# A one-core f32 transformer pair: every stage's two operand tiles begin at other bytes

## The chip, the cores and the metric

The kernel runs on one NeuronCore of one Trainium2 chip. The metric is the device time in microseconds of one execution, lower is better.

## The reference, cut to what matters

Two blocks run one after the other on a sequence of 256 tokens with 1,024 features, all in f32. What matters here is that nearly all work is a matrix product with a large weight, and that most products read one normalised activation.

```python
# first block
h = rmsnorm(x, g_mix[l]); proj = h @ w_in[l]          # attention, LRU, memory, gates
merged = g0*(attn_out @ p_attn) + g1*(lru_out @ p_lru) + g2*(mem_out @ p_mem)
x = x + merged @ w_out[l]
h2 = rmsnorm(x, g_ffn[l])
q = (h2 @ w_peer_q) ...                                # top-16 experts of 16384 per head
act = gelu(einsum('chkd,cd->chk', u_tab[ix], hx)); out = einsum('chk,chkd->cd', gx*act, v_tab[ix])
# second block, layer 0: gated_deltanet_bidir; layer 1: dilated_window_attention
for i in range(2):
    x = x + mixer_i(rmsnorm(x, norm_mix[i]))
    h = rmsnorm(x, norm_mlp[i]); x = x + square(relu(h @ w1[i])) @ w2[i]
return rmsnorm(x, norm_final)
```

The kernel computes the expert layer densely: all 16,384 rows of `peer_u` and of `peer_v` pass through TensorE, and the gates pick from the result.

## The kernel before, in words

Activations lie feature-major: a tile `[128, 8, 256]` holds 8 slices (`kt`) of 128 features by T = 256 tokens, so one slice is 1,024 bytes in each partition. Every product is made of three f32r matmuls (`mm3`, L445): both factors are split in a high and a low part, and high·high, high·low and low·high are added in PSUM. The *stationary* operand of a matmul is a 128 x 128 piece of a weight (`whi`, `wlo`, made from `wraw` by ACT at L202 and by DVE or POOL at L206 and L204, streamed from HBM by SP); the *moving* operand is a slice of an activation tile, 256 columns. `gemm_y` (L453) runs over the 8 slices of one activation tile for one output tile `mmps`; `gemm_k` (L486) keeps one slice as the moving operand and fills 8 outputs in the four `acc` banks. The only exceptions among the big products are `d_v`, `w_va` and `w_vm`: there a piece of the weight moves (256, 384 or 512 columns) and the activation stands.

The activation's two parts lie in the pool `opr` under two tags, `xhi` and `xlo`, one buffer each, 8,192 bytes in each partition. Stage after stage takes the same two buffers under other names: `xhi/xlo` (input projections and gates, here stage A), `qhi/qlo` (queries of the experts, Q), `bhi/blo` (`peer_u`, U), `chi/clo` (`peer_v`, V), `ghi/glo` (gated delta net, G), `mxh/mxl` (the two MLPs, M0 and M1), `dxh/dxl` (dilated attention, D), and at the very end `y`. Other moving operands are tiles of their own: `rh/rl` in the second product of an MLP, `yhl` in the output product of the delta net, and the branch results that give `p` and `acc<-mg` in the first block (also called `bhi/blo` there, with output `p`). The stage's tiles are written by `split` (L438): ACT writes the high part (L439), DVE the low part (L441, or L443 with the norm's gain). In stage V the eight slices are rewritten in turn while the products run.

In the program as built, `xhi` begins at byte 67,680 of a partition and `xlo` at byte 75,872. Both are 96 modulo 128 and also 96 modulo 256, and so is every slice, a slice being 1,024 bytes. `whi` and `wlo` begin at 64 modulo 256. `rh`, `rl`, `yhl` and `mg` begin at 160 modulo 256, the branch results of `p` and the tiles of `acc<-dohi` at 32 modulo 256 (all of these are 32 modulo 128).

Of the kernel before, what the change touches and what calls it, by code (L numbers as in the profile page):

```python
# [10 lines left out]
F32 = mybir.dt.float32  # L11
F32R = mybir.dt.float32r
# [10 lines left out]
T = 256  # L23
# [339 lines left out]
def build(tc, a, out, stop=None, dbg=None):  # L363
# [3 lines left out]
    with ctx:  # L367
# [5 lines left out]
        opr = ctx.enter_context(tc.tile_pool(name="opr", bufs=1))  # L373
# [64 lines left out]
        def split(hi, lo, src, scale=1.0):  # L438
            S.activation(hi, src, AF.Copy, scale=scale)  # L439
            if isinstance(scale, float) and scale == 1.0:  # L440
                return V.tensor_sub(lo, src, hi.bitcast(F32)).ins  # L441
            else:
                return V.scalar_tensor_tensor(lo, src, scale, hi.bitcast(F32), op0=ALU.mult, op1=ALU.subtract).ins  # L443

        def mm3(o, whi_, wlo_, xhi_, xlo_, start, stop):  # L445
            mm(o, whi_, xhi_, start, False)
            mm(o, whi_, xlo_, False, False)
            mm(o, wlo_, xhi_, False, stop)

        def aux(nm="aux"):  # L450
            return aux_p.tile([128, 512], F32, name=nm, tag="aux")

        def gemm_y(key, X, kts=range(8), ps=None, first=True, last=True):  # L453
            hi, lo = st.get(key) if key is not None else st.of
            if ps is None:
                ps = mm_p.tile([128, 512], F32, name="mmps", tag="mm")[:, :T]
            kts = list(kts)
            for j, kt in enumerate(kts):
                w = slice(kt * 128, (kt + 1) * 128)
                mm3(ps, hi[:, w], lo[:, w], X[0][:, kt, :], X[1][:, kt, :],  # L460
                    first and j == 0, last and j == len(kts) - 1)
            return ps

        def start(keys, X, after, between, bank=None, half=4):

            ps = [gemm_y(keys[0], X)]
            c = after()
            ps.append(gemm_y(keys[1], X, range(half), last=False))
            r = between(c)
            gemm_y(None, X, range(half, 8), ps[1], first=False)  # L470
            return ps + [gemm_y(keys[2], X, ps=(aux("y3") if bank is None else bank)[:, :T])], r

        def acc_new():
            return [q for _ in range(2) for q in acc_two()]
# [11 lines left out]
        def gemm_k(key, xh, xl, acc, first, last):  # L486
            hi, lo = st.get(key)
            for n in range(8):
                w = slice(n * 128, (n + 1) * 128)
                o = acc[n // 2][:, (n % 2) * T:(n % 2) * T + T]  # L490
                mm3(o, hi[:, w], lo[:, w], xh, xl, first and n % 2 == 0, last)

        def gemm_k2(keys, xs, acc):

            ws = [st.get(k, i == 0) for i, k in enumerate(keys)]
            for n in range(8):
                w = slice(n * 128, (n + 1) * 128)
                o = acc[n // 2][:, (n % 2) * T:(n % 2) * T + T]
                for i in range(2):
                    mm3(o, ws[i][0][:, w], ws[i][1][:, w], *xs[i], False, i == 1)  # L500


        ident = const.tile([128, 128], F32, name="ident")
        make_identity(nc, ident)
# [88 lines left out]
        def plus(x, acc, scale=None):  # L593

            def upd(n):
                q = acc[n // 2][:, (n % 2) * T:(n % 2) * T + T]
                if scale is None:
                    V.tensor_add(x[:, n, :], q, x[:, n, :])
                else:
                    V.scalar_tensor_tensor(x[:, n, :], q, scale, x[:, n, :], op0=ALU.mult, op1=ALU.add)  # L600

            pending.append(upd)

        def operand(x, gname, X, nm, ahead={}):

            N = Norm(nm)
            for kt in range(8):
                update(kt)
                N.lo = split(X[0][:, kt, :], X[1][:, kt, :], x[:, kt, :], col(gname, kt))
                N.add(x[:, kt, :], kt)  # L610
                if kt in ahead:
                    st.pump(cut=ahead[kt])
            return N
# [8 lines left out]
        with ExitStack() as pa:  # L622
# [9 lines left out]
            for i in range(2):  # L632
                nc.sync.dma_start(out=x0[:, 4 * i:4 * i + 4, :], in_=a["xT"][:, 4 * i:4 * i + 4, :])
            st.pump(split=False)
            hx = (opr.tile([128, 8, T], F32R, name="xhi", tag="xhi"), opr.tile([128, 8, T], F32R, name="xlo", tag="xlo"))
            posi = lp.tile([32, T], I32, name="posi", tag="gt", bufs=NG + 1)
            nc.gpsimd.dma_start(out=posi, in_=bass.AP(tensor=a["pos"].tensor, offset=a["pos"].offset, ap=[[0, 32], [1, T]]))
            amask = A1.tile([128, 2, T], F32, name="amask")
# [178 lines left out]
            for c in range(2):  # L817
                hi, lo = st.get(("w_va", c))
                for j in range(4):
                    kt = c * 4 + j  # L820
                    w = slice(j * 256, (j + 1) * 256)
                    for t in range(2):
                        o = vps[:, t * 256:(t + 1) * 256]
# [64 lines left out]
            for n in range(8):  # L888
# [8 lines left out]
                for j in range(8):  # L897
                    w = slice(j * 128, (j + 1) * 128)
                    o = p01[:, :T] if j < 6 else p01[:, T:]
                    mm3(o, hi[:, w], lo[:, w], bo[0][:, j, :], bo[1][:, j, :], j in (0,), j == 5)  # L900
                hi, lo = st.get(("p_all", 2 * n + 1))
                for j in range(8):
                    kt = 8 + j
                    w = slice(j * 128, (j + 1) * 128)
                    o = p01[:, T:] if kt < 12 else p2[:, :T]
# [28 lines left out]


        x1d = dram.tile([128, 8, T], F32, name="x1d")
        hq = (opr.tile([128, 8, T], F32R, name="qhi", tag="xhi"), opr.tile([128, 8, T], F32R, name="qlo", tag="xlo"))
        N = operand(x1, "g_ffn", hq, "ssb")
        nc.gpsimd.dma_start(out=x1d, in_=x1)
        with ExitStack() as pb:  # L940
# [8 lines left out]
            for n in range(16):  # L949
                ps = p3[n] if n < 3 else gemm_y(("w_peer_q", n), hq)  # L950
                V.tensor_mul(qT[:, n, :], ps, rb)
            hb = (opr.tile([128, 8, T], F32R, name="bhi", tag="xhi"), opr.tile([128, 8, T], F32R, name="blo", tag="xlo"))
            for t in range(2):
                for g in range(4):
                    p = aux("sc")
# [144 lines left out]
            bg.drain()  # L1100
            bg.add(scatter(1))
            acc = acc_new()
            cq = (opr.tile([128, 8, T], F32R, name="chi", tag="xhi"), opr.tile([128, 8, T], F32R, name="clo", tag="xlo"))
            cz = []
            for c in range(128):
                if c < 126:
# [23 lines left out]
        with ExitStack() as pc:  # L1130
            C1p = pc.enter_context(tc.tile_pool(name="C1", bufs=1))
            cp = pc.enter_context(tc.tile_pool(name="cp", bufs=2))
            gcs = pc.enter_context(tc.tile_pool(name="gcs", bufs=1))
            hx = (opr.tile([128, 8, T], F32R, name="ghi", tag="xhi"), opr.tile([128, 8, T], F32R, name="glo", tag="xlo"))
            tri = gcs.tile([128, 2, 128], F32, name="tri")
            nc.gpsimd.dma_start(out=tri, in_=a["tri"])

# [405 lines left out]
            for c, h in gorder:  # L1543
# [9 lines left out]
                elif c == "v":  # L1553
                    vf = cp.tile([128, T], F32, name="vf", tag="vf")
                    conv(ps, 16 + h, vf)
                    p = aux("vT")
# [34 lines left out]


        def mlp(i):
            hx = (opr.tile([128, 8, T], F32R, name="mxh", tag="xhi"), opr.tile([128, 8, T], F32R, name="mxl", tag="xlo"))
            N = operand(xr, f"norm_mlp{i}", hx, "ssf")
            acc = acc_new()
            with tc.tile_pool(name="mp", bufs=3) as mp:
                todo = []

                def second():  # L1600
                    n, h, l = todo.pop(0)
                    gemm_k((f"w2_{i}", n), h, l, acc, n == 0, False)

                p3, r2 = start([(f"w1_{i}", n) for n in range(3)], hx, N.sums, lambda c: N.rows(c, "rstd"), half=(YD, YF)[i])
                for n in range(32):
                    ps = p3[n] if n < 3 else gemm_y((f"w1_{i}", n), hx)
                    if n >= LA:
                        second()
                    r = mp.tile([128, T], F32, name="r", tag="r")
                    V.scalar_tensor_tensor(r, ps, 0.0, r2, op0=ALU.max, op1=ALU.mult)  # L1610
                    S.activation(r, r, AF.Square)
                    rh, rl = (mp.tile([128, T], F32R, name=x, tag=x, bufs=LA + 1) for x in ("rh", "rl"))
                    split(rh, rl, r)
                    todo.append((n, rh, rl))
                while len(todo) > 2:
                    second()
                gemm_k2([(f"w2_{i}", n) for n in (30, 31)], [q[1:] for q in todo], acc)
            plus(xr, acc)

        mlp(0)  # L1620
        if stop == "D":
            flush()
# [4 lines left out]
        with ExitStack() as pd:  # L1627
            D1 = pd.enter_context(tc.tile_pool(name="D1", bufs=1))
            dp = pd.enter_context(tc.tile_pool(name="dp", bufs=2))
            hx = (opr.tile([128, 8, T], F32R, name="dxh", tag="xhi"), opr.tile([128, 8, T], F32R, name="dxl", tag="xlo"))  # L1630
            N = operand(xr, "norm_mix1", hx, "ssd", DA)

            vv = D1.tile([128, 2, 1152], F32, name="vv")
# [20 lines left out]
            for j in range(2):  # L1654
                p = aux("trc")
# [16 lines left out]
            for w in (slice(0, 512), slice(512, 768)):  # L1672
                p = aux("bias")
                p = p[:18, :w.stop - w.start]
# [121 lines left out]
        if stop == "E":  # L1796
            flush()
            nc.sync.dma_start(out=out, in_=xr)
            return
        mlp(1)  # L1800
        N = Norm("ssf", V, ND)
        y = opr.tile([128, 8, T], F32, name="y", tag="xhi")
        for kt in range(8):
            update(kt)
            N.add(xr[:, kt, :], kt)
# [32 lines left out]
```

## Time and profile before

| | us |
|---|---|
| median of two runs (1946.83 to 1948.34) | 1947.59 |
| the profiled execution, its own time | 1948.6 |
| its span, first to last instruction | 1946.8 |
| time around the span | 1.8 |
| PE busy | 1851.0 (95%) |
| DVE busy | 1416.4 (73%) |
| ACT busy | 975.0 (50%) |
| mean granted TensorE clock | 0.982 |

How to read it: in a dense stretch each matmul overlaps the next, so its own duration (some 280 ns) is not what it costs. What it costs is the distance from its start to the next one's start, here called the *pace*: a stretch of the chain of waits divided by its matmuls.

### The profile page before, as it was taken

What the parts mean: (1) busy time and instruction counts of PE and PEld (TensorE: products, weight loads), DVE (VectorE), ACT (ScalarE), POOL (GpSimd) and SP (SyncE); (2) the same over time, 40 slices, a digit from 0 to 9 for tenths busy, and PEclk for the clock granted to TensorE, in tenths of its full rate; (3) what the DMA queues carried; (4) which work ended last, traced back from release to release, by engine and by line L of the source; (5) the groups of instructions that cost most, each with busy time, mean ns of one, the idle gap of its engine ahead of it and who ended that gap; (6) DMA issues with size and microseconds to landing.
All of it is one profiled execution on the core that took longest, in us unless ns stands there. A gap on an engine that the chain in (4) does not pass through costs nothing.

```text
span 1946.8 us, 38503 instructions
## 1 busy us (share of the span) xinstructions
PE 1851.0 (95%) x15622; PEld 1812.2 (93%) x15622; DVE 1416.4 (73%) x2644; ACT 975.0 (50%) x1589; POOL 347.5 (18%) x202
## 2 busy tenths in 40 slices
PE   8999999999989999999999997669999999999998
PEld 7989999999989999999999996668899999999998
DVE  7698666877778887999865559997565556766555
ACT  6577444544443334444354454634754546455543
POOL 2010001343433332000000045552130001010000
PEclk9999999999999999999999998889999999999999
DMA  6534556455554445545565662344145566645653
GB/s 225 184 121 141 184 185 208 154 170 181 170 170 152 151 153 162 164 154 162 162 204 188 188 215 80 95 100 104 44 151 184 184 185 204 195 131 184 185 186 108
DMA packets 113703, 314.85 MB, mean 162 GB/s; under 512 B 35042, under 2 KB 38242, under 8 KB 112758
## 3 DMA queue, kind: packets, MB, share of 16 engines
q1 hardware_dynamic: 112390, 305.82, 49.9%
q0 software_dynamic: 1136, 6.59, 1.0%
q8 instruction: 122, 2.00, 0.4%
q14 instruction: 55, 0.45, 0.1%
HBM read 307.06 MB, written 5.30 MB: 160 GB/s over the span
## 4 chain that ended last, share of the span: by engine, by line
PE 80%; DVE 14%; issue 2%; ACT 2%; DMA 0%; POOL 0%; DVEq 0%; SPq 0%; ACTq 0%; POOLq 0%
PE mmps L434 36%; PE acc L434 34%; PE gp L434 3%; DVE cy L1254 3%; DVE wlo L206 2%; PE p L434 2%; PE vps L434 1%; ACT whi L202 1%; DVE U L1291 1%; DVE kv L1337 1%; DVE mxl L443 1%; PE lg L434 1%; DVE tk L1034 1%; PE po L434 0%; DVE tk L1033 0%
## 5 line engine op out<-in xcount | busy, mean ns | idle before, releaser
L202 ACT ACTIVATE whi<-wraw 128x1024 fp32r<-128x1024 f32 x562 | 595.7, 1060 | 785.2 <-PE acc L434 299.6
L206 DVE TENSOR_TENSOR wlo<-wraw,whi 128x1024 fp32r<-128x1024 f32 x461 | 577.7, 1254 | 315.2 <-ACT whi L202 313.3
L204 POOL TENSOR_TENSOR wlo<-wraw,whi 128x1024 fp32r<-128x1024 f32 x101 | 248.8, 2464 | 694.3 <-ACT whi L202 629.0
L434 PE MATMUL mmps<-bhi,wlo 128*128 128x256 f32 x1024 | 286.6, 280 | 8.0 <-DVE wlo L206 7.7
L434 PE MATMUL mmps<-bhi,whi 128*128 128x256 f32 x1024 | 288.8, 282 | 3.7 <-ACT act L1089 3.7
L434 PE MATMUL mmps<-blo,whi 128*128 128x256 f32 x1024 | 286.3, 280 | 0.0
L434 PE MATMUL acc<-chi,whi 128*128 128x256 f32 x1008 | 283.2, 281 | 0.0
L434 PE MATMUL acc<-clo,whi 128*128 128x256 f32 x1008 | 281.2, 279 | 0.3 <-DVE clo L441 0.3
L434 PE MATMUL acc<-chi,wlo 128*128 128x256 f32 x1008 | 280.9, 279 | 0.0
L434 PEld LDWEIGHTS mmps<-bhi,wlo 128*128 128x128 f32 x1024 | 192.5, 188 | 9.4 <-DVE wlo L206 8.7
L434 PEld LDWEIGHTS mmps<-bhi,whi 128*128 128x128 f32 x1024 | 193.2, 189 | 4.3 <-ACT act L1089 4.3
L434 PEld LDWEIGHTS mmps<-blo,whi 128*128 128x128 f32 x1024 | 192.5, 188 | 0.0
L434 PEld LDWEIGHTS acc<-clo,whi 128*128 128x128 f32 x1008 | 189.6, 188 | 0.6 <-DVE clo L441 0.5
L434 PEld LDWEIGHTS acc<-chi,whi 128*128 128x128 f32 x1008 | 189.9, 189 | 0.0
L434 PEld LDWEIGHTS acc<-chi,wlo 128*128 128x128 f32 x1008 | 189.5, 188 | 0.0
L434 PE MATMUL acc<-rl,whi 128*128 128x256 f32 x512 | 144.6, 283 | 0.0
L434 PE MATMUL acc<-rh,wlo 128*128 128x256 f32 x512 | 144.5, 282 | 0.0
L434 PE MATMUL acc<-rh,whi 128*128 128x256 f32 x512 | 143.1, 280 | 0.0
L434 PE MATMUL mmps<-mxl,whi 128*128 128x256 f32 x496 | 140.3, 283 | 1.3 <-DVE mxl L443 1.0
L434 PE MATMUL mmps<-mxh,wlo 128*128 128x256 f32 x496 | 139.6, 281 | 0.8 <-DVE wlo L206 0.8
L434 PE MATMUL mmps<-mxh,whi 128*128 128x256 f32 x496 | 138.9, 281 | 0.8 <-ACT mxh L439 0.5
L434 PE MATMUL mmps<-xhi,whi 128*128 128x256 f32 x384 | 111.3, 290 | 1.7 <-DVE qm L860 1.2
(576 smaller groups left out, 4474.2 us busy)
## 6 DMA issues: line engine op xcount, KB each, us to landing
wraw<-in_peer_u SPq DMA_DIRECT2D x128, 512.0 KB, 3.6
wraw<-in_peer_v SPq DMA_DIRECT2D x128, 512.0 KB, 3.9
wraw<-in_w SPq DMA_DIRECT2D x128, 512.0 KB, 4.3
wraw<-in_w_gates SPq DMA_DIRECT2D x24, 512.0 KB, 3.5
wraw<-in_p_all SPq DMA_DIRECT2D x16, 512.0 KB, 3.6
wraw<-in_w_peer_q SPq DMA_DIRECT2D x16, 512.0 KB, 3.6
wraw<-in_d_v SPq DMA_DIRECT2D x12, 512.0 KB, 4.4
wraw<-in_d_q SPq DMA_DIRECT2D x9, 512.0 KB, 4.3
```

The lines of the kernel that those rows point to most:

```text
L202: nc.scalar.activation(hi, t, AF.Copy)
L204: nc.gpsimd.tensor_tensor(lo, t, hi.bitcast(F32), op=ALU.subtract)
L206: self.lasts.append(nc.vector.tensor_sub(lo, t, hi.bitcast(F32)).ins)
L434: x = PE.matmul(o, l, r, start=start, stop=stop, skip_group_check=True)
L443: return V.scalar_tensor_tensor(lo, src, scale, hi.bitcast(F32), op0=ALU.mult, op1=ALU.subtract).ins
L1034: V.tensor_tensor(eq.rearrange("p (h k) c -> p h k c", h=2), eq.rearrange("p (h k) c -> p h k c", h=2), tif4[:, h:h + 2, p2, None, :].to_b ...
L1254: V.scalar_tensor_tensor(y[:, lo_:hi_], x[:, lo_ + d:hi_ + d], col("gdn_conv", j * 24 + base), y[:, lo_:hi_], op0=ALU.mult, op1=ALU.add)
L1291: V.scalar_tensor_tensor(U[:, u, :], kk[:, h, t, :], rk2b[:, t, d, h:h + 1], D[:, u, :], op0=ALU.mult, op1=ALU.mult)
L1337: V.tensor_tensor(q, M[:, 0:i, 0:i].rearrange("p j c -> p c j"), L[:, i, None, 0:i].to_broadcast([128, i, i]), op=ALU.mult)
```

## The change

A new helper `operands(names, at)` takes the same two buffers, each 32 elements (128 bytes) longer, and returns views that begin `at` bytes in. Each stage calls it with two offsets of its own, all multiples of 4. `y` takes the longer buffer and begins where it did. In the core of the diff below the seven calls stand for the seven lines that they replace.

```diff
+        def operands(names, at):
+            r = []
+            for nm, tag, o in zip(names, ("xhi", "xlo"), at):
+                t = opr.tile([128, 8 * T + 32], F32R, name=nm, tag=tag)
+                r.append(t[:, o // 4:o // 4 + 8 * T].rearrange("p (k t) -> p k t", t=T))
+            return tuple(r)
-            hx = (opr.tile([128, 8, T], F32R, name="xhi", tag="xhi"), opr.tile([128, 8, T], F32R, name="xlo", tag="xlo"))
+            hx = operands(("xhi", "xlo"), (112, 120))
+        hq = operands(("qhi", "qlo"), (16, 24))
+            hb = operands(("bhi", "blo"), (8, 4))
+            cq = operands(("chi", "clo"), (48, 80))
+            hx = operands(("ghi", "glo"), (64, 36))
+            hx = operands(("mxh", "mxl"), ((0, 16), (12, 20))[i])
+            hx = operands(("dxh", "dxl"), (104, 100))
-        y = opr.tile([128, 8, T], F32, name="y", tag="xhi")
+        y = opr.tile([128, 8 * T + 32], F32, name="y", tag="xhi")[:, :8 * T].rearrange("p (k t) -> p k t", t=T)
```

In the program as built the instructions, their order on every engine and their semaphores are the same. The first buffer still begins at byte 67,680; the second moves by 128 bytes to 76,000, and whatever lies behind it in the partition moves by 256 bytes, which leaves its place modulo 256 as it was. The stages' slices then begin here (before: 96 and 96 everywhere):

| stage | matmuls on its tiles | high part, modulo 256 (128) | low part, modulo 256 (128) |
|---|---|---|---|
| A `xhi/xlo` | 1,152 | 208 (80) | 88 (88) |
| Q `qhi/qlo` | 384 | 112 (112) | 248 (120) |
| U `bhi/blo` | 3,072 | 104 (104) | 228 (100) |
| V `chi/clo` | 3,024 | 144 (16) | 48 (48) |
| G `ghi/glo` | 792 | 160 (32) | 4 (4) |
| M0 `mxh/mxl` | 768 | 96 (96) | 240 (112) |
| D `dxh/dxl` | 432 | 200 (72) | 68 (68) |
| M1 `mxh/mxl` | 768 | 108 (108) | 244 (116) |

## Rows read from the trace of the kernel before

**Rows 1.** The page: engines' busy time and instructions; TensorE's granted clock, 40 slices.
```profile
PE 1851.0 (95%) x15622; PEld 1812.2 (93%) x15622; DVE 1416.4 (73%) x2644; ACT 975.0 (50%) x1589; POOL 347.5 (18%) x202
PEclk9999999999999999999999998889999999999999
```

**Rows 2.** The page: the chain that ended last, shares by engine, then by line.
```profile
PE 80%; DVE 14%; issue 2%; ACT 2%; DMA 0%; POOL 0%; DVEq 0%; SPq 0%; ACTq 0%; POOLq 0%
PE mmps L434 36%; PE acc L434 34%; PE gp L434 3%; DVE cy L1254 3%; DVE wlo L206 2%; PE p L434 2%; PE vps L434 1%; ACT whi L202 1%; DVE U L1291 1%; DVE kv L1337 1%; DVE mxl L443 1%; PE lg L434 1%; DVE tk L1034 1%; PE po L434 0%; DVE tk L1033 0%
```

**Rows 3.** Busy time in stretches: A, U, V, G, M0; then clock and DMA.
```profile
core 0: us, PE busy (x) PEld busy (x) DVE busy (x) ACT busy (x) POOL busy (x), PEclk, DMA share, GB/s
34.00:238.00 204.00, 198.41 (x1501) 189.49 (x1500) 162.41 (x328) 130.88 (x227) 10.61 (x8) 0.98 0.50 159
...
339.00:754.00 415.00, 402.92 (x3645) 399.11 (x3644) 327.53 (x787) 183.50 (x275) 158.67 (x64) 1.00 0.50 162
755.00:1141.00 386.00, 385.71 (x3528) 384.19 (x3526) 289.14 (x468) 174.57 (x259) 7.54 (x3) 1.00 0.56 178
1147.00:1389.00 242.00, 191.24 (x1492) 181.85 (x1492) 199.05 (x431) 126.27 (x271) 105.92 (x56) 0.89 0.36 100
1424.00:1612.00 188.00, 186.67 (x1547) 185.50 (x1546) 109.77 (x143) 96.14 (x144) 8.46 (x8) 0.99 0.57 180
```

**Rows 4.** Groups by line and tile, one product of three per stage: busy, mean, idle before.
```profile
L434 PE MATMUL mmps<-bhi,whi 128*128 128x256 f32 x1024 | 288.8, 282 | 3.7 <-ACT act L1089 3.7
L434 PE MATMUL acc<-chi,whi 128*128 128x256 f32 x1008 | 283.2, 281 | 0.0
L434 PE MATMUL mmps<-mxh,whi 128*128 128x256 f32 x496 | 138.9, 281 | 0.8 <-ACT mxh L439 0.5 <-DVE r L1610 0.3
L434 PE MATMUL mmps<-xhi,whi 128*128 128x256 f32 x384 | 111.3, 290 | 1.7 <-DVE qm L860 1.2 <-DVE m L910 0.4
L434 PE MATMUL mmps<-ghi,whi 128*128 128x256 f32 x256 | 79.3, 310 | 9.1 <-DVE cx L1249 9.1
L434 PE MATMUL mmps<-dxh,whi 128*128 128x256 f32 x144 | 41.2, 286 | 0.0
L434 PE MATMUL mmps<-qhi,whi 128*128 128x256 f32 x120 | 33.7, 282 | 0.3 <-ACT qhi L439 0.3
```

**Rows 5.** The chain in order of time, M0: start us, length us, what, matmuls.
```profile
1446.58 2.88 PE acc L434 x24
1449.46 2.83 PE mmps L434 x24
1452.29 2.88 PE acc L434 x24
```

**Rows 6.** The chain elsewhere: `p`, U twice, V's second half, `yhl`, `d_v`.
```profile
229.58 5.67 PE p L434 x48
...
353.62 57.87 PE mmps L434 x490
...
461.72 51.66 PE mmps L434 x443
...
972.33 182.40 PE acc L434 x1560
...
1412.67 15.85 PE acc L434 x132
...
1640.95 8.55 PE vps L434 x48
```

**Rows 7.** The chain at a plain f32 product of 256 columns, stage A.
```profile
65.01 0.86 PE lg L434 x4
```

**Rows 8.** Groups by line: the two writers of stage V's tiles; DVE in an MLP's.
```profile
L441 DVE TENSOR_TENSOR clo<-act,chi 128x256 fp32r<-128x256 f32 x126 | 51.9, 418 | 0.0
L439 ACT ACTIVATE chi<-act 128x256 fp32r<-128x256 f32 x126 | 49.1, 400 | 1.4 <-DVE act L1083 1.4
L443 DVE SCALAR_TENSOR_TENSOR mxl<-xr,cols,mxh 128x256 fp32r<-128x256 f32 x16 | 12.7, 812 | 0.5 <-ACT mxh L439 0.5
```

More of the change, by code (lines that the diff above doesn't have):

```diff
@@ L936, in build @@
         x1d = dram.tile([128, 8, T], F32, name="x1d")
-        hq = (opr.tile([128, 8, T], F32R, name="qhi", tag="xhi"), opr.tile([128, 8, T], F32R, name="qlo", tag="xlo"))
+        hq = operands(("qhi", "qlo"), (16, 24))
         N = operand(x1, "g_ffn", hq, "ssb")
@@ L951, in build @@
                 V.tensor_mul(qT[:, n, :], ps, rb)
-            hb = (opr.tile([128, 8, T], F32R, name="bhi", tag="xhi"), opr.tile([128, 8, T], F32R, name="blo", tag="xlo"))
+            hb = operands(("bhi", "blo"), (8, 4))
             for t in range(2):
@@ L1102, in build @@
             acc = acc_new()
-            cq = (opr.tile([128, 8, T], F32R, name="chi", tag="xhi"), opr.tile([128, 8, T], F32R, name="clo", tag="xlo"))
+            cq = operands(("chi", "clo"), (48, 80))
             cz = []
@@ L1133, in build @@
             gcs = pc.enter_context(tc.tile_pool(name="gcs", bufs=1))
-            hx = (opr.tile([128, 8, T], F32R, name="ghi", tag="xhi"), opr.tile([128, 8, T], F32R, name="glo", tag="xlo"))
+            hx = operands(("ghi", "glo"), (64, 36))
             tri = gcs.tile([128, 2, 128], F32, name="tri")
@@ L1593, in mlp @@
         def mlp(i):
-            hx = (opr.tile([128, 8, T], F32R, name="mxh", tag="xhi"), opr.tile([128, 8, T], F32R, name="mxl", tag="xlo"))
+            hx = operands(("mxh", "mxl"), ((0, 16), (12, 20))[i])
             N = operand(xr, f"norm_mlp{i}", hx, "ssf")
@@ L1629, in build @@
             dp = pd.enter_context(tc.tile_pool(name="dp", bufs=2))
-            hx = (opr.tile([128, 8, T], F32R, name="dxh", tag="xhi"), opr.tile([128, 8, T], F32R, name="dxl", tag="xlo"))
+            hx = operands(("dxh", "dxl"), (104, 100))
             N = operand(xr, "norm_mix1", hx, "ssd", DA)
```

## The prediction

> **What bounds the kernel now.** I read the page's engine line first, then the shares of the chain, then the busy time by stage, and last the chain in order of time, from which the pace comes. [...] The chain that ends last is PE for 80%, and `mmps` and `acc`, the two outputs of the big products, make 70% [rows 2]. By stage the bound is clear where most matmuls are: in U PE works 402.9 of 415 us, in V 385.7 of 386, in M0 186.7 of 188, in A 198.4 of 204. Only in G does it idle, 191 of 242 us, with DVE at 199 [rows 3]. So a change of the pace of matmuls reaches the end almost undiminished in every stage but G, and what ACT, DVE and the DMAs do in between is covered.
>
> The paces are the key. In M0 the chain alternates between two products of the same form: 24 matmuls that write `mmps` take 2.83 us, 117.9 ns each, and 24 that write `acc` take 2.88 us, 120.0 ns each [rows 5]. Clock, sizes, types and the weights' buffers are the same. What differs is the output bank pattern and the start of the moving operand: `mxh/mxl` begin at 96 modulo 256, `rh/rl` at 160. The output pattern is not it: in V, which also writes `acc` but whose slices begin at 96, 1560 matmuls take 182.40 us, 116.9 ns each [rows 6]. And `yhl`, at 160, writes `acc` at 15.85 us for 132, 120.1 ns [rows 6]. So the byte at which a moving operand begins already costs up to 3 ns in 117 in this trace. That 32 modulo 128 is not one class shows too: `p`, at 32 modulo 256, has 5.67 us for 48, 118.1 ns [rows 6], between the two. The start 64 appears where a weight piece of 384 columns moves: 8.55 us for 48 `vps`, 178.1 ns, or 118.7 per 256 columns [rows 6]. So four starts are known, 96, 32, 64 and 160, with 116.6 to 118.1, 118.1, 118.7 and 120.0 ns. At one and the same start the pace also has two values: U runs 490 matmuls in 57.87 us (118.1 ns) and later 443 in 51.66 us (116.6 ns) [rows 6].
>
> **The change part by part.** No instruction is added, removed or moved, no byte more is transferred, and no wait changes; the two buffers grow by 128 bytes a partition. All that can cost is access to the shifted tiles.
>
> *Moving reads.* The groups count 1024, 1008, 496, 384, 256, 144 and 120 matmuls for one of the three products of `mm3` [rows 4]; three times their sum is 10,296 (96 more stand in small groups). G's 768 are left out, for there DVE and not PE ends the chain. In M0 the high part keeps its start, 96, so its 496 (two products of 248) cost nothing. 10,296 - 768 - 496 = 9,032 matmuls read at a new start. What they cost there the trace shows for none of the new starts but G's 160. From below: nothing, or a gain; 96 is the best start of four, but nothing says that it is the best of all. From above, without a new mechanism: the 120.0 ns of the start 160. I take the mean of the three other known starts, since the new ones are spread over the whole 256 bytes: (118.1 + 118.7 + 120.0) / 3 = 118.9 ns. The old pace over U, V and M0 is about 117.1 ns (116.6 and 118.1 in U, 116.9 in V, 117.9 in M0). The difference is 1.8 ns, and 9,032 x 1.8 ns = 16 us. The two paces of U put some 0.75 ns on either side, 7 us.
>
> *Writes and other reads of the shifted tiles.* ACT writes and DVE reads and writes 256 columns at a time: 400 and 418 ns in V, 812 ns in an MLP's norm where DVE waits for ACT [rows 8]. V's 126 pairs have idle engines around them (DVE 289, ACT 175 of 386 us [rows 3]). On the path lie only the seven norms with 8 pairs each; if each pair became 5% slower, (0.4 + 0.8) us x 56 x 0.05 = 3 us. No row shows such a cost, and the shifted f32 elements still lie whole in their 4 bytes, so I take 0.
>
> *Stationary reads.* In D, parts of `dxh/dxl` stand instead of moving. These loads overlap the matmuls before them (PEld 1812 us beside PE's 1851 [rows 1]), and I take 0.
>
> The sum, made against the profiled execution: 1948.6 + 16 = 1965 us. That execution lies 1.0 us above the median of 1947.6; I let the 1 us stand, as it is far inside the spread. If the cover of DVE and ACT were missing the 3 us would come on top.
>
> [...]
>
> **The rivals.**
> *No effect (1943 to 1953 us).* The difference between 96 and 160 could come from where `rh` and `yhl` lie in the partition or how far the parts are from each other, not from the low bits. For it: one start has two paces in U. Against it: `rh`, `yhl` and the output product in the first block lie far apart and all begin at 160. It gives 1948.
>
> *One more piece per slice (slower).* If PE fetches a slice in fixed pieces, a start inside a piece needs one piece more. All four known starts are multiples of 32, so no row speaks against pieces of up to 32 bytes; pieces of 64 would have made 96, 32 and 160 dearer than 64 by a sixteenth, 7.3 ns, which they are not. With 32-byte pieces each of nearly all 9,032 matmuls pays 116.9 / 32 = 3.7 ns, 33 us: 1948.6 + 33 = 1982, and with the 16 us of the spread 1998. With pieces of 16 bytes only those in U, M1, D and the low parts of A and Q pay (some 4,800 matmuls), 1.8 ns each: 9 us, 1957 to 1974. Beyond 39 us, 4.3 ns each, it is slower by over 2%. [...]
>
> *The fast rate is lost (much slower).* A start that is a multiple of 4 but not of 8 could break the pace of f32r. The nearest row is plain f32, where each matmul of 256 columns takes 0.86 us / 4 = 215 ns [rows 7], 98 ns more. Four modulo 8 are the low parts of U (1,024), D (144) and both parts of M1 (744): 1,912 x 98 ns = 187 us, 2136 us. For it speaks only that no moving operand at such a start stands in the trace.
>
> *A gain (faster).* If the new starts were as much better than 96 as 160 is worse, 9,032 x 3.1 ns = 28 us come off: 1920. [...] Faster by over 2% needs -4.3 ns per matmul. Against it: all three other known starts are worse than 96.
>
> **How the numbers follow.** My forecast, a small loss between 1953 and 1980 us: 0.45. No effect: 0.20. A gain: 0.10, of which 0.03 by over 2%. One more piece at 32 bytes, 1980 to 2005: 0.20, of which 0.15 beyond 2% (1986.5). The fast rate lost: 0.05. With 0.02 for a larger spread than seen, slower by over 2% has 0.22, faster 0.03, and 0.75 stay within 2%, about what a measurement of this kernel can tell from no change. The range goes down into the gains, to 1942, and up through most of the 32-byte case, to 2000; below it is about 0.08, above it about 0.12. The likeliest case's own range is 1953 to 1980.
>
> **What would show it.** The chain in order of time gives the pace of each stage again. Right: U, V, A, Q, D and M1 between 117 and 120 ns, V (two thirds of its matmuls at 144) and U setting the sum, M0 least changed, `rh/rl` as before at 120.0, `p` at 118.1, G's chain still DVE's. A uniform 120.5 or more in every stage with starts off a multiple of 32 is the piece rival; stages at 4 modulo 8 near 215 ns for their shifted products are the lost rate; unchanged paces are the first rival. The forecast is wrong if the paces move by different amounts for the same class of start, or if the span moves without them.

## The result, and the profile after

The changed kernel takes 1966.47 us (median of two runs, 1965.88 to 1967.05) against 1947.59 us: ratio 1.0095, 95% interval 1.0076 to 1.0114. That is 18.9 us or 1% slower; 1965 had been forecast. The profiled execution has 1965.88 us and a span of 1964.1 us, 17.3 us more than the span of before.

The page after, with the engines' busy time and the granted clock, is to be set beside [rows 1]:

```profile
PE 1875.8 (96%) x15622; PEld 1835.8 (93%) x15622; DVE 1414.4 (72%) x2644; ACT 974.6 (50%) x1589; POOL 347.6 (18%) x202
PEclk9999999999999999999999998889999999999998
```

The chain of waits after, in order of time (start us, length us, what, matmuls): `p`, U twice, V's second half, `yhl`, then M0 twice, `d_v`, M1 three times; it is to be set beside [rows 5, 6]:

```profile
229.57 5.67 PE p L434 x48
...
354.21 76.19 PE mmps L434 x634
...
464.04 70.41 PE mmps L434 x587
...
985.10 185.70 PE acc L434 x1560
...
1425.68 15.85 PE acc L434 x132
...
1460.95 2.83 PE mmps L434 x24
1463.78 2.88 PE acc L434 x24
...
1652.36 8.42 PE vps L434 x48
...
1768.59 3.83 PE mmps L434 x17
...
1865.77 2.85 PE mmps L434 x24
1868.63 2.88 PE acc L434 x24
```

The other engines worked as long as before, and PE 25 us longer with the same 15,622 matmuls. U now runs at 76.19 / 634 = 120.2 and 119.9 ns a matmul (118.1 and 116.6 before), V at 119.0 (116.9). What the change did not touch stands still to the second decimal: `p` 5.67 us for 48, `yhl` 15.85 for 132, `rh/rl` 2.88 for 24. M0's own product, whose high part keeps its start, has 2.83 for 24 as before.

The stages' lengths, from the first matmul of each stage to the first of the next, tell where the 17 us arose. The pace beside them is the mean distance between starts of all matmuls on the stage's two tiles, distances over 135 ns (a wait) left out:

| stage | length before, us | after | difference | pace before, ns | after |
|---|---|---|---|---|---|
| A | 252.6 | 252.6 | 0.0 | 116.8 | 117.1 |
| Q | 52.0 | 52.7 | +0.7 | 117.8 | 119.9 |
| U | 416.6 | 425.4 | +8.9 | 116.9 | 120.3 |
| V | 392.3 | 398.9 | +6.6 | 116.7 | 118.9 |
| G | 276.8 | 273.8 | -3.1 | 117 | 118.9 |
| M0 | 187.9 | 186.4 | -1.5 | 117.7 | 118.0 |
| D | 127.9 | 129.0 | +1.1 | 117 | 120.8 |
| M1 | 189.6 | 194.3 | +4.7 | 116.6 | 119.1 |

Not all of it is pace. Busy time by stretch after (columns as in [rows 3]); V, G, M0, M1 and M1's first 47 us:

```profile
765.00:1164.00 399.00, 398.71 (x3581) 397.04 (x3580) 291.78 (x470) 177.35 (x261) 7.54 (x3) 1.00 0.55 175
1164.00:1438.00 274.00, 227.37 (x1772) 216.17 (x1772) 216.64 (x471) 147.88 (x316) 122.17 (x69) 0.91 0.35 95
1438.00:1624.00 186.00, 184.68 (x1543) 183.54 (x1542) 110.03 (x144) 95.67 (x144) 8.43 (x8) 1.00 0.58 182
...
1753.00:1947.00 194.00, 192.75 (x1574) 191.22 (x1574) 111.00 (x147) 98.47 (x148) 8.45 (x8) 0.98 0.51 164
...
1753.00:1800.00 47.00, 45.75 (x345) 44.22 (x345) 28.91 (x45) 25.88 (x46) 8.45 (x8) 0.93 0.43 136
```

V is as full as before (398.7 of 399 us), so its pace passes whole to the end. In M1 the granted clock is 0.50 for a while at the norm: the chain there has 17 matmuls in 3.83 us, 225 ns each, where before, at 1.00, it had

```profile
1755.41 2.10 PE mmps L434 x17
```

Before, such a dip lay in M0 (0.99 over the stage [rows 3], 0.59 over 14 matmuls that take 2.87 us, 205 ns each), and in the kernel after M0 has 1.00. So M1 pays some 3 us and M0 gains 1 to 2 that have nothing to do with the operand's place. In G, where PE idles 47 of 274 us, the dearer pace (118.9 against 117) is not seen in the length at all.

### The profile page after: what moved, and what is told of

It reads as the page before. It is cut to its first block, busy times and chain, and to the rows that moved or that the text cites. A ratio compares the mean times of both kernels' runs of the same rounds, so it can differ in the third digit from the quotient of the medians.

```text
span 1964.1 us, 38503 instructions
## 1 busy us (share of the span) xinstructions
PE 1875.8 (96%) x15622; PEld 1835.8 (93%) x15622; DVE 1414.4 (72%) x2644; ACT 974.6 (50%) x1589; POOL 347.6 (18%) x202
## 4 chain that ended last, share of the span: by engine, by line
PE 83%; DVE 13%; ACT 2%; issue 2%; DMA 0%; DVEq 0%; SPq 0%; ACTq 0%
PE mmps L434 38%; PE acc L434 34%; PE gp L434 3%; DVE cy L1262 3%; DVE wlo L206 2%; PE p L434 2%; PE vps L434 1%; DVE U L1299 1%; ACT whi L202 1%; DVE mxl L443 1%; DVE kv L1345 1%; PE lg L434 1%; PE po L434 0%; DVE tk L1042 0%; DVE tk L1041 0%
## 5 line engine op out<-in xcount | busy, mean ns | idle before, releaser
L434 PE MATMUL mmps<-bhi,wlo 128*128 128x256 f32 x1024 | 292.5, 286 | 7.3 <-DVE wlo L206 7.3
L434 PE MATMUL mmps<-bhi,whi 128*128 128x256 f32 x1024 | 293.2, 286 | 3.3 <-ACT act L1097 3.3
L434 PEld LDWEIGHTS acc<-clo,whi 128*128 128x128 f32 x1008 | 189.6, 188 | 0.6 <-DVE clo L441 0.5
```

The source lines that it names most:

```text
L434: x = PE.matmul(o, l, r, start=start, stop=stop, skip_group_check=True)
```

## The experiments

All kernels take the two buffers longer and the helper of the change; a third argument of `operands` is the extra distance between slices in elements, so that V's eight slices can have eight starts. The edits below show the lines that matter; `...` marks lines left out. Starts are given modulo 256; where nothing else is said the weights' parts stay at 64 and high and low part begin at the same place. Each kernel's paces are worked out as in the table above, V's for each slice alone (some 370 matmuls each).

### A grid of 32 bytes, a grid of 4 bytes

`e1_grid32`; the lines of U and V stand here for those of all stages:

```diff
-            hb = operands(("bhi", "blo"), (8, 4))
+            hb = operands(("bhi", "blo"), (64, 64))
...
-            cq = operands(("chi", "clo"), (48, 80))
+            cq = operands(("chi", "clo"), (0, 0), 8)
```

> Both parts of a stage begin at the same byte modulo 256 here, all of them multiples of 32: A 128, Q 0, U 160, M0 64, M1 192, D 224, and stage V's eight slices at 96, 128, 160, 192, 224, 0, 32, 64. The weights stay at 64. Theory 1 (the pace is a property of the start modulo 256): U near 120.0 ns, the pace of rh and yhl at 160, against 116.9 before; V's slices differ among each other, 96 at 116.7, 160 at 120.0, 32 near 118.2, 64 near 118.5; M0 near 118.5. Theory 2 (the pieces: only a start off a multiple of 32, or 16, costs): all stages and all slices within 1 ns of 117. Theory 3 (not the start but the place of rh and yhl in the partition): likewise all at 117, rh at 120. Time: about 1948 us by theories 2 and 3; by theory 1 U alone adds 3072 x 3.1 ns = 9.5 us, V about 1.5 ns on 3024 = 4.5 us, together some 1960 to 1966.

`e2_grid4` is made the same way, with U at 104 and V's slices 4 bytes apart:

```diff
+            hb = operands(("bhi", "blo"), (8, 8))
...
+            cq = operands(("chi", "clo"), (0, 0), 1)
```

> Fine steps: stage V's eight slices begin at 96, 100, 104, 108, 112, 116, 120, 124 modulo 256, and the other stages, both parts alike, at A 200, Q 88, U 104, M0 208, M1 112, D 68. Theory 1 (a property of the start modulo 256, single bytes included): the paces of the changed kernel come back start by start wherever they stand, 104 near 121.6 ns in U and in V's third slice, 112 near 120.6 in M1 and V's fifth, 200 near 120.6 in A, 208 near 116.9 in M0, 68 near 121 in D. Theory 2 (pieces of 16 bytes): V's slices at 96 and 112 alike at 116.7 ns, the six others 1.8 ns higher and alike; with pieces of 32 bytes seven slices alike, 3.7 ns above 96. Theory 4 (what counts is the pair of the high and the low part's starts, 104 with 228 in the changed kernel): U at 104 with 104 far from the 120.3 ns that its stage had. Time: by theory 1 U adds 3072 x 4.5 ns = 14 us, V some 2 ns x 3024 = 6 us, M1 and A 3 to 4 us: 1968 to 1974; by theory 2 at 16 bytes 1955 to 1960.

Measured: 1957.85 us and 1967.18 us (before beside them: 1948.17). V's slices, ns a matmul:

| e1: start | 0 | 32 | 64 | 96 | 128 | 160 | 192 | 224 |
|---|---|---|---|---|---|---|---|---|
| ns | 114.2 | 118.2 | 119.6 | 118.0 | 117.6 | 119.5 | 118.7 | 117.8 |

| e2: start | 96 | 100 | 104 | 108 | 112 | 116 | 120 | 124 |
|---|---|---|---|---|---|---|---|---|
| ns | 116.9 | 121.2 | 120.2 | 117.7 | 118.4 | 120.3 | 119.8 | 116.7 |

The time of e1 lies just below the 1960 to 1966 us expected, that of e2 just below its 1968 to 1974. What follows: the pace depends on the start down to 4 bytes. Pieces of 32 bytes are out: 124, 108 and 208 (M0 in e2 118.9) lie within such a piece and cost no more than 64. The lost fast rate is out too: at 4 modulo 8 the dearest is D at 68 in e2 with 123.1 ns, nowhere near 215. And 96 is not the best: Q at 0 in e1 runs at 113.6 ns.

### Everything 64 bytes further

`e3_shift` puts 64 bytes ahead of all tiles, so the weights begin at 128; the operands of U, V, Q and G move along (96 to 160), those of A, M0, M1 and D stay at 96:

```diff
+        const.tile([128, 16], F32, name="shift")
...
+            hb = operands(("bhi", "blo"), (0, 0))
...
+            hx = operands(("dxh", "dxl"), (192, 192))
```

> Everything in the partition behind the first few tiles lies 64 bytes further on, the weights' two parts included (128 instead of 64 modulo 256). U, V, Q and G keep their old distance to the weights and so begin at 160; A, M0, M1 and D are put back to 96, 32 bytes ahead of the weights' start instead of 32 behind it. rh and yhl lie at 224, p at 96. Theory R (the distance between moving and stationary operand counts, as where two reads meet): U and V stay at 116.9 and 116.7 ns, rh at 120.0, p at 118.2; M0, M1 and A change, to about 118.2, the pace that the distance of -32 had in p. Time about 1948 to 1951 us. Theory 1 (the moving start by itself): U and V go to 120.0 ns, p to 117, rh to what the first scan shows at 224 (117 to 118), M0, M1, A and D stay at 117. Time 1948 + (3072 + 3024) x 3.1 ns = 1967, less 4 us in rh.

Measured: 1952.86 us. The chain, U twice and V's second half:

```profile
355.40 57.87 PE mmps L435 x490
...
463.57 51.66 PE mmps L435 x443
...
975.33 182.40 PE acc L435 x1560
```

These three lengths are those of before to the last digit [rows 6], though every tile begins 64 bytes later and the operand at 160, the start that cost 120.0 in [rows 5]. A, M0, M1 and D, at 96 as before but with the weights at 128, went from 116.6 to 117.7 up to 118.2 and 118.3 ns, the pace that `p` (32, weights at 64) has. So it is not the moving operand's start alone: the start of the standing weights counts as well, and 64 bytes on both together change nothing. U and V carry this; the rise in A, M0, M1 and D is not much more than the 1.1 ns between the two levels that one pair of starts can have (next section).

### One stage alone

`e4_u_alone` gives U its two starts of the change (104 and 228) and all other stages 96:

```diff
+            hb = operands(("bhi", "blo"), (8, 132))
...
+            cq = operands(("chi", "clo"), (0, 0))
```

> Only U has its new starts (104 and 228 modulo 256), every other stage begins at 96 with both parts. If the stages add up, each by its own pace: U at 120.3 ns instead of 116.9, 3072 x 3.4 ns = 10.4 us, of which the stage lengths of the two traces show 8.9; the time 1956 to 1958 us against 1947.6, ratio 1.0045 to 1.0055, and V, M1 and D as before. If the loss came from where the buffers behind the operand tiles lie, or from the stages together, the ratio would be 1.000 or 1.009.

Measured: 1957.74 us (1956.06 to 1958.34), ratio 1.0052, interval 1.0032 to 1.0072. The chain, U and V:

```profile
351.54 76.21 PE mmps L434 x634
...
979.07 184.06 PE acc L434 x1560
```

U has its 76.2 us for 634 as in the changed kernel and is 8.8 us longer, as U is there (8.9); V is back at 117.2 over the stage, with 118.0 in this stretch. U's cost comes through whole when U alone has it; the ratio of 1.009 expected from a common cause did not come.

V here shows something else. Its starts and those of its weights are the ones of before (96 and 64), yet this stretch takes 184.06 us where [rows 6] have 182.40, and V is 1.7 us longer. Taken block by block (24 matmuls on one slice), V has 116.7 ns in its first half and 117.8 in its second, and before it has 116.7 in both. U before begins at 117.8 and stands at 116.7 from about the thirtieth of its 128 blocks on; M0 and M1 have 117.7 and 116.6 before, and 116.6 and 117.7 here. So one pair of starts can have two paces, 1.1 ns apart, and it keeps either for hundreds of matmuls. Nor is that scatter: over a thousand matmuls without a gap in V's second half, the three matmuls of one product take 350.0 ns before, 353.3 in e4 and 356.7 in the changed kernel. What sets the level isn't shown. Differences of about 1 ns between two kernels therefore don't tell two starts apart, while those of 3 ns and more do.

### Where the cheap starts lie

`e5_grid16` sets V's slices to the other multiples of 16 and the stages close above 0; `e6_near0` looks finer around 0.

```diff
+            hb = operands(("bhi", "blo"), (160, 160))
...
+            cq = operands(("chi", "clo"), (16, 16), 8)
```

> The odd multiples of 16: stage V's eight slices begin at 112, 144, 176, 208, 240, 16, 48, 80 modulo 256 (both parts alike); U at 0, the one start that was clearly better than 96 (114.1 ns in V and 113.6 in Q of the first scan); A 4, Q 8, M0 252, M1 248, D 12, all close to 0. Theory R with 256-byte periods (the distance to the weights' start, 64, sets the pace, and -64 is a place where the two reads miss each other): U near 114 ns, 3072 x 2.8 = 9 us off; A, Q, M0, M1 and D each between 112 and 118, lower the nearer they are to the good distance; 112 in V at 118.4 as in the fine scan. The rival (the low pace at 0 belongs to a start on a 256-byte boundary itself, a whole number of pieces, and not to the distance): U at 114 as well, but A at 4, Q at 8, M0 at 252, M1 at 248 and D at 12 lose all of it at once and stand at 118 or more. Time: with U at 114 and the rest near 118, about 1946 to 1952 us.

```diff
+            hb = operands(("bhi", "blo"), (140, 140))
...
+            cq = operands(("chi", "clo"), (136, 136), 2)
```

> Steps of 8 around 0: stage V's eight slices at 232, 240, 248, 0, 8, 16, 24, 32 modulo 256; U 236, A 244, Q 20, M0 16, M1 28, D 176. By the distance to the weights the pace falls from some 118 at 232 to 114 or less near 0 and comes back to 118.2 at 32, over several neighbouring starts; by the rival (a whole number of pieces only at 0) the slice at 0 stands alone at 114 among seven at 118 to 120. Time 1946 to 1960 us.

Measured: 1956.72 us (before beside it 1949.43) and 1965.28 us, both above the times expected (up to 1952 and 1960), since the starts around the cheap 0 came out dear. V's slices:

| e5: start | 16 | 48 | 80 | 112 | 144 | 176 | 208 | 240 |
|---|---|---|---|---|---|---|---|---|
| ns | 119.0 | 117.4 | 115.4 | 118.2 | 119.1 | 114.4 | 118.7 | 119.4 |

| e6: start | 232 | 240 | 248 | 0 | 8 | 16 | 24 | 32 |
|---|---|---|---|---|---|---|---|---|
| ns | 120.0 | 119.2 | 120.1 | 114.9 | 120.1 | 119.1 | 121.5 | 118.2 |

The stages close to 0 in e5 (starts 4, 8, 12, 248 and 252) have 118.3 to 121.7 ns. So there is neither a smooth hollow around 0 nor a single boundary: three lone starts, 0, 80 and 176, are 3 ns cheaper than their neighbours on the grid of 16. D at 176 in e6 has 114.2 again. These means mix V's two halves; in the first, where the products `gp` come between some of its blocks, the cheap starts are dearer (80: 117.1, then 114.0; 176: 115.0, then 113.7). Over the four kernels e1, e2, e5 and e6, multiples of 16 lie between 114 and 120 ns (mean about 118), 8 modulo 16 between 119 and 121.5, 4 modulo 16 between 120 and 123, 12 modulo 16 between 116.7 and 120.

### The cheap start everywhere, and in the two tiles alone

`e8_all176` puts every moving operand at 176, also `rh/rl`, `yhl`, `mg`, the branch results and `dohi/dolo`; `e12_two_tiles` moves the two tiles of each stage only and leaves out the rest:

```diff
+            hb = operands(("bhi", "blo"), (80, 80))
...
+                    rh, rl = (mp.tile([128, T + 64], F32R, name=x, tag=x, bufs=LA + 1)[:, 4:4 + T] for x in ("rh", "rl"))
...
+            mg = A1.tile([128, 8 * T + 64], F32R, name="mg", tag="r12")[:, 4:4 + 8 * T].rearrange("p (a b t) -> p a b t", a=4, b=2)
```

> Weights at 64 as before; every moving operand of the big products at 176 modulo 256: the two tiles of all stages, and also rh/rl, yhl, mg (160 before) and the branch results of p and acc<-dohi (32 before). By the single looks 176 has 114.2 to 114.4 ns in two stages. If 176 holds in all stages: U 3,072 x 2.6 + V 3,024 x 2.3 + A, Q, M0, D, M1 3,500 x 2.7 + rh/rl, yhl, mg some 2,000 x 5.7 + the others 2 us, some 38 us, 1910 us, ratio 0.980. Rival: DVE, ACT or the weights' stream then end more of the waits (before: U 403 of 415 us busy, A 198 of 204), and only a part comes through, 1915 to 1930, ratio 0.984 to 0.991. Rival: the low pace of 176 was of those two stages or of the other parts' places and not of the start: paces of 117, 1945, ratio 0.998.

> Only the two operand tiles at 176 in every stage; rh/rl, yhl, mg, the branch results and dohi/dolo back at their starts of before (a part of e8_all176). The parts add up: e8 gave 39 us; the 1,536 matmuls of rh/rl at 6.7 ns, yhl, mg, p and dohi at 4 to 6 ns are some 15 us of these, which come back: 1924 us, ratio 0.988 (0.986 to 0.990), and paces of 114 in the stages, 120 for rh/rl. Rival: the other tiles' starts cost nothing and the gain of e8 was all in the two tiles: 1909.

Measured: e8 1908.33 us (1906.55 to 1910.22), ratio 0.9806, interval 0.979 to 0.9822, the best kernel of this study. e12 1922.05 us (1920.22 to 1927.54), ratio 0.9877, interval 0.9853 to 0.9902. The page of e8, then its chain: U twice, V, M0:

```profile
PE 1808.0 (95%) x15622; PEld 1769.1 (93%) x15622; DVE 1416.2 (74%) x2644; ACT 976.2 (51%) x1589; POOL 351.2 (18%) x202
```

```profile
352.18 60.16 PE mmps L434 x528
...
452.38 50.28 PE mmps L434 x444
...
956.48 177.49 PE acc L434 x1560
...
1446.48 2.72 PE mmps L434 x24
1449.20 2.72 PE acc L434 x24
```

And the chain of e12, V and M0:

```profile
959.41 177.48 PE acc L434 x1560
...
1447.36 2.88 PE acc L434 x24
1450.24 2.72 PE mmps L434 x24
```

The pair of M0 shows it on four rows: 2.83 and 2.88 before, 2.72 and 2.88 with the two tiles moved, 2.72 and 2.72 with `rh/rl` moved too, 113.3 ns where it was 120.0. With weights at 64, start 176 gives 113.3 to 115.7 ns in every stage. Both times came out as summed from the paces (1910 and 1924 expected); no other engine takes over, DVE stands at 74%.

### The weights 8 and 16 bytes further

Is it the distance between the two starts alone? `e7_weights8` moves the weights to 72, `e10_weights16` to 80; in both the ring of raw weights is one tile shallower (3 instead of 4) to make room.

```diff
-            hi = self.his.tile([128, 1024], F32R, name="whi", tag="whi")
+            hi = self.his.tile([128, 1088], F32R, name="whi", tag="whi")[:, 2:1026]
```

> Weights' parts begin 8 bytes later (72 modulo 256 instead of 64; for that the ring of raw weights is 3 deep instead of 4), and each stage has high and low part at one start: U 104, A 96, M0 8, M1 0, D 184, Q 112, V's eight slices 96, 104 ... 152. Theory of the distance (only moving start minus stationary start counts, modulo 256): U is 32 behind its weights, as 96 was, so 116.9 ns; A (24, as 88) 120; M0 (-64, as 0 was) 114.5; M1 (-72, as 248) 119.7; D (112, as 176) 114.2; V 96: 120.1, 104: 116.8, 112: 120.2, 120: 118.4, 128: 119.8, 136: 117.6. Theory of the start's own place in 16 bytes (multiples of 16 cheap, 8 modulo 16 dear, wherever the weights lie): U 119.5 to 120, A 117, M0 120, M1 115, D 120, V 96 117 and 104 120. rh/rl (160, distance 88, as 152): by distance 120 or a little more, by own place 120.0.

```diff
+            hi = self.his.tile([128, 1088], F32R, name="whi", tag="whi")[:, 4:1028]
```

> Weights' parts begin 16 bytes later (80 modulo 256; the ring of raw weights 3 deep instead of 4). High and low part at one start: A 176, Q, U, D 192, M0 176, M1 96, V's slices 224, 240, 0, 16, 32, 48, 64, 80. Theory of the distance in whole steps of 16 bytes (each start acts as the one 16 bytes lower did before weights at 64): U, Q, D 192 as 176: 114.2; A, M0 176 as 160: 120; M1 96 as 80: 115.4; V 118.7, 117.9, 119.4, 114.5, 119, 118.2, 117.9, 119.6. Theory of the own place: U, Q, D 118.7; A, M0 114.2; M1 116.8; V 117.9, 119.4, 114.5, 119, 118.2, 117.9, 119.6, 115.4. rh/rl (160): by distance as 144, 119; by own place 120.0.

Measured: 1953.67 and 1957.50 us. Paces, with what each theory expected:

| kernel, place, start | measured, ns | by distance | by own place |
|---|---|---|---|
| e7 U 104 | 120.2 | 116.9 | 119.5 to 120 |
| e7 A 96 | 117.9 | 120 | 117 |
| e7 M0 8 | 121.2 | 114.5 | 120 |
| e7 D 184 | 123.4 | 114.2 | 120 |
| e7 Q 112 | 113.5 | 119.3 to 120.2 | 118.3 |
| e7 V 112 | 114.5 | 120.2 | 118.3 |
| e7 M1 0 | 118.2 | 119.7 | 115 |
| e10 A, M0 176 | 119.8, 119.4 | 120 | 114.2 |
| e10 V 16 | 114.2 | 114.5 | 119 |
| e10 V 0 | 118.8 | 119.4 | 114.5 |
| e10 U 192 | 119.1 | 114.2 | 118.7 |
| e10 V 32 | 123.2 | 119 | 118.2 |
| e10 M1 96 | 117.4 | 115.4 | 116.8 |

One row from each chain, M0 in e7 (120.8 ns) and a stretch of U in e10 (120.3):

```profile
1446.71 2.90 PE mmps L434 x24
```

```profile
357.12 60.41 PE mmps L434 x502
```

Both theories fall. `rh/rl`, at 160 in both kernels, say the same: 118.6 ns in e7 and 118.1 in e10, where both theories had 119 or more. By 8 bytes the order of cheap and dear follows mostly the operand's own place in 16 bytes, but a new cheap start appears, 112. By 16 bytes the start 176 loses its low pace and the cheap 0 moves along to 16, while the cheap 176 does not move to 192. Only this stands: the pace belongs to the pair of starts, and a pair must be measured.

### Who meets whom

`e9_no_prep` takes e5's starts for V and 160 for U, and leaves out the preparation of weights in half of U and half of V (which blocks, the expectation says); their products use the parts made last.

```diff
+        def none(i):
+            name, c = self.plan[i][0]
+            return (name == "peer_u" and 64 <= c < 128) or (name == "peer_v" and 4 <= c < 64)
...
+            if none(self.ns):
...
+                self.s[self.ns] = self.kept
```

> Part of the work left out: the 64 last blocks of peer_u are neither loaded nor split (their products take the parts of block 63 again), blocks 4 to 63 of peer_v are loaded but not split. U's tiles begin at 160, V's slices at 16, 48, 80 ... 240 as in e5_grid16. Theory one (TensorE's own two reads, moving and stationary, meet in the memory): the paces stay: U 120.0 in both halves, V 119.0, 117.4, 115.4, 118.2, 119.0, 114.4, 118.7, 119.4 in both halves. Theory two (TensorE's reads meet those and the writes of DVE, ACT, POOL or of the DMAs on the weights): in U's second half, where none is left, and largely in V's first half, the paces of all starts fall to the 113 to 114.5 of start 176, and come back in V's second half. If only V's first half stays dear, it is the DMAs alone.

Measured: 1959.25 us. Busy time by stretch (columns as in [rows 3]): U's first half, U's second, V's first, V's second:

```profile
360.00:540.00 180.00, 175.06 (x1449) 173.81 (x1447) 138.17 (x469) 87.53 (x128) 74.08 (x30) 1.00 0.54 170
560.00:755.00 195.00, 195.00 (x1860) 193.44 (x1859) 105.54 (x239) 21.65 (x56) 0.00 (x0) 1.00 0.50 160
790.00:970.00 180.00, 180.00 (x1718) 178.80 (x1718) 104.23 (x240) 21.41 (x51) 0.00 (x0) 1.00 0.01 1
985.00:1150.00 165.00, 165.00 (x1406) 165.00 (x1406) 93.09 (x124) 82.51 (x124) 6.99 (x2) 1.00 0.61 189
```

The transfers of the blocks that are loaded but not split ran ahead, through U's second half; in V's first half there is then none (0.01), POOL has no instruction and ACT works 21 of 180 us. The paces did not fall: U 119.98 and 119.94 ns in its halves; V's slices in the first half 119.0, 117.4, 116.6, 118.3, 118.3, 115.2, 118.6, 119.6 and in the second 119.0, 117.4, 114.0, 118.2, 119.6, 113.7, 118.8, 119.2 (starts 16, 48 to 240). e5, with all the preparation, has the same difference between its halves at 80 and 176, so the first half is dearer there with or without it. So the DMAs, POOL and ACT don't set these paces; they stayed, as theory one has it, but its cause, two reads that meet, isn't shown by that. DVE, with 104 of 180 us, was still there, so this kernel does not take its part away. The traces do, though: in V's second half before (980 to 1145 us), the 692 distances between starts during which DVE works throughout average 116.67 ns, the 604 during which it idles 116.70; in e8 (965 to 1130 us) it is 113.31 over 758 and 113.33 over 558. DVE's work beside a matmul doesn't change the pace either. Where the loaded weights begin does: M0 and A at 176 have 119.4 and 119.8 ns with weights at 80 (e10), 113.5 and 114.3 with weights at 64 (e8), and U and V at 160 have 116.6 to 118.1 ns with weights at 128 (e3), where U at 160 has 119.94 to 119.98 with weights at 64 (e9).

### Two starts in one stage

The change gives each stage two starts; e1 to e8 mostly one. `e11_mixed` mixes starts whose paces were known alone:

```diff
+            hb = operands(("bhi", "blo"), (0, 64))
...
+            cq = operands(("chi", "clo"), (80, 0))
```

> Weights at 64 as before, high part / low part at two different starts, each known from stages where both parts began there: A 160/96, Q 176/160, U 96/160, V 176/96, M0 176/0, M1 0/176, D 176/96. Two of three products read the high part. Theory one (each matmul has the pace of its own start, so different starts cost nothing in themselves): A (2 x 120 + 117) / 3 = 119, Q 116.2, U 118.0, V 115.1, M0 114.3, M1 114.4, D 115.1; time 1948 - V 5 + U 3 + A 2 - M0, M1 2 x 2 = 1944. Theory two (a change between starts costs in itself): 1 ns and more above these in all stages, 1953 and over, and M0 and M1 not below 115.5 although both their starts are cheap ones.

Measured: 1955.56 us (before beside it 1948.87). The chain, U, V and M0:

```profile
354.41 57.89 PE mmps L434 x490
...
981.21 184.04 PE acc L434 x1560
...
1457.95 2.78 PE mmps L434 x24
```

U (96/160) 117.9 where 118.0 was the mean of its two starts, A (160/96) 118.3 where 119: no extra cost. But V (176/96) has 119.2 where the mean is 115.1. Its halves differ: in the first, with `gp` between, it has 121.1, with whole blocks at 124.2, worse than either start alone; in the second 117.8, which 96 alone has too at its higher level (e4). D with the same starts has 118.9 (96 alone 117 before, 176 alone 114.2 in e6), Q (176/160) 117.9 where 116.2, and M0 and M1, mixed from the two cheap starts 0 and 176, 116.2 and 115.7 where 114.3 and 114.4 were the means. The time, 1955.56 us, is that of theory two (1953 and over) and not the 1944 of theory one, but A and U show no cost. So neither theory holds everywhere: a matmul's pace also depends on the starts of its neighbours. It works the other way too: in the changed kernel A's 208 with 88 runs at 117.1, though each alone has 118.8 and 120.1 in other stages.

## Why the prediction was right

**What bounds it.** Right. V's 6.7 us of pace (3,024 x 2.2 ns) became 6.6 of length, U's 10.4 (3,072 x 3.4) became 8.9, and G's became none. e4, e8 and e12 show the same: the times came out as summed from the paces.

**The 1.8 ns.** The term was too small: 2.4 ns were measured, a third more. By the table, U and V give 10.4 + 6.7 us, A, Q, D and M1 0.3 + 0.8 + 1.6 + 1.9, M0 0.2: 21.9 us over 9,032 matmuls, 2.4 ns and not 1.8. Over the six stages U, V, A, Q, D and M1 the pace went from 116.8 to 119.3 ns, where the sum had 117.1 and 118.9. The span took only 17.3: G and M0 gave back 3.1 and 1.5, U's waits 1.5, and M1 lost some 3 to the clock. So the forecast's 16 beside the 17.3 is in part luck: errors of a few us on both sides cancel. G's -3.1 isn't explained; its length lay between 11.4 us below and 5.5 above that of before in these kernels.

**The reason given for it.** Here a step failed, though the time came out. The prediction took the moving operand's start as what counts, and the mean of three other starts as a fair draw. e3 refutes the first: 160 costs 116.9 once the weights stand at 128. `mxh` and `rh` in [rows 5] differ by their place against the weights, which the prediction did not look at. The prediction's own sign of error, the same class of start with different paces, came true: each distance counted to the matmul that it begins with, 104 has 121.6 in U of the changed kernel beside 228, and 119.3 in e2 beside 104. U as a whole (120.3) and D (120.8) also lie above the 117 to 120 named as the sign of being right, and A (117.1) hardly moved. What sets a pace, as far as the runs show it, is the pair of starts, the starts of the neighbours and a level that can differ at the same starts. The draw was fair all the same: with weights at 64 the four classes modulo 16 of e1 to e6 average some 118, 120, 121 and 118 ns, together 119, and the forecast's 118.9 is that mean, while 96, at 116.8, lies below it.

**Writes and stationary reads at nothing.** Right. The two writers of V's tiles after (instructions, shortest, middle and longest ns, from and to us), which answer to [rows 8]:

```profile
L439 ACT ACTIVATE chi<-act x126: 395/403/420, 772.3 to 1143.1; 128x256 fp32r<-128x256 f32 x126
L441 DVE TENSOR_TENSOR clo<-act,chi x126: 404/417/444, 773.5 to 1144.4; 128x256 fp32r<-128x256 f32 x126
```

403 and 417 ns beside 400 and 418. In D, `d_v` reads its `dxh/dxl` standing: 8.42 us for 48 beside 8.55, so nothing was lost there.

**The rivals.** No effect fell with U's 120.2. Pieces of 32 bytes and the lost rate fell with e2. Of 16-byte pieces something is left, since starts off a multiple of 16 are dearer on the mean, but 124 (116.7) is cheaper than 112 (118.3), so not as a fixed cost of each start inside a piece. The gain was possible all along, only not with these starts: e8 has it, 39 us, with paces at 113 to 114. The lowest over a long stretch of its chain is 50.28 us for 444, 113.2 ns, and the measurements leave a spread of 10 ns, 113 to 123, to the place.

## What to carry to other kernels

Where matmuls follow each other without a gap, their pace is in part a property of the layout (113 to 123 ns in these kernels): work it out per product from the chain (length by matmuls), and where two products of one form differ, compare the low bits of both operands' addresses, the moving and the standing one. Cheap places can't be computed from a rule known here, but they can be scanned, eight in one kernel by spacing the slices, and then all moving operands put at the one that is cheap against the weights; high and low part at the same one. Trust differences of 3 ns, not of 1: equal starts alone can differ by 1.1 ns.

## What the runs showed of the hardware

- For 256 f32r columns at a granted clock of 1.00 the pace lies between 113 and 123 ns, by where in 256 bytes the moving and the standing operand begin (weights at 64: 176, 0 and 80 cheap, 113.3 to 115.7 ns on the mean; 68, 4, 24, 200, 244 and 100 dear, 121 ns and more).
- A shift of both by 64 bytes left it unchanged in U and V (e3: 57.87, 51.66 and 182.40 us, three times the same length); a shift of both by 8 or 16 did not in U (e7: 120.2 ns at 104, 116.9 at 96 before; e10: 119.1 at 192, 113.9 and 113.2 at 176 in e8).
- The same pair of starts (96, weights at 64) has two paces, 116.7 and 117.8 ns, each kept over hundreds of matmuls (V in e4: one half each). For the three matmuls of one product the steady lengths in V's second half are 340.0, 350.0, 353.3 and 356.7 ns (e8, before, e4, after). What sets the level stays open.
- The pace stays with no DMA, no POOL and little ACT beside it (e9: V's first half; U 119.98 and 119.94 ns), and is the same beside a working and an idle DVE (before: 116.67 and 116.70 ns). What sets it, beyond the starts of TensorE's two operands and of their neighbours, was not shown.
- It depends on the neighbours: two operands at different starts that alternate can be slower than either alone (e11, D at 176 and 96: 118.9; alone 114.2 and 117).
- A dip of the granted clock to 0.5 at an MLP's norm lies in M0 before (14 matmuls in 2.87 us) and in M1 after (17 in 3.83 us), and is worth 1.5 to 3 us as an estimate from these stages' lengths: differences as small between single profiles should not be read.
